# A hybrid decoder block in one kernel: the SSD branch's norm moved beside GLA, its CB mask, z product and transfer order changed

## The chip, the cores and the metric

The kernel runs on one core of a Trainium2 chip. The core has five engines with an instruction queue each: TensorE (PE) for matmuls and transposes, VectorE (DVE), ScalarE (ACT), GpSimd (POOL) and SyncE (SP), which here only issues transfers (DMA). Each engine takes its queue strictly in order; a wait at its head holds all that is behind it. The metric is the device time of one execution in microseconds. Lines such as L51 are lines of the kernel before.

## What is computed

A decoder block over 1024 tokens with a width of 1024, all in float32. Two branches read the same normed input and are merged, then come attention to a memory of 256 tokens and a gated feed-forward layer. The change concerns the first branch, the SSD (Mamba-2) mixer, and the stage of the second (GLA, gated linear attention):

```python
proj = n @ w_in
z, xBC, dt_raw, q, k, v, r, a1, g_ssd, g_gla = split(proj)
# SSD: B, C for 2 groups of 8 heads, 128 states; x has 16 heads of 64
xBC = silu(conv(xBC));  xs, Bm, Cm = split(xBC)
y = sum over s <= l of (C_l . B_s) * exp(a_cs_l - a_cs_s) * (x_s dt_s)   # plus the carried state
y = (y + D_skip * xs) * silu(z)
y_ssd = y * rsqrt(mean(y*y over each group of 512 channels) + EPS) * ssd_norm
y_gla = gla(q, k, v, r, a1, ...)
merged = sigmoid(g_ssd) * (y_ssd @ w_up_ssd) + sigmoid(g_gla) * (y_gla @ w_up_gla)
h = h + merged @ w_o
```

## The kernel before, in words

**Layout.** All activations stand transposed: channels on the 128 partitions, tokens along the row. Float32 precision comes from a split of every matmul operand into a high and a low part (`whi`, `wlo`, B11h, B11l and so on): ACT writes the high part (L220), DVE subtracts it from the source for the low one (L221), and three matmuls are made of each product.

**Units.** The projection by `w_in` is cut into units of 256 output channels. A unit (class Unit, L272) loads 1 MB of weights (`raw`, L286), and makes seven block products in the manner of Strassen, named B11, T2, T1, B21, T3, B22, T4 in the order of SPACED (L40). Each is 12 matmuls of 128x512 into one accumulator of PSUM (`acc`, four of them). A product's result is moved or added into `o` by ACT (L349, L351) or DVE, and the finished quarters are stored (`store_rows`, L465). The units come in the order zu (z, silu, stored in `sz_d`), xu (convolution), ru, qk, gs, gg. `singles` (L454) runs units one after another and gives each the next one to load; `group` asks for it at product n ≥ `frm`, which was always 6.

**Fillers.** `run` (L433) draws a generator of side work at a given rate between the products. Beside ru, qk and gs0 stands the SSD scan (391 to 640 us), beside gs1 to gg2 the GLA scan (645 to 790 us). The order of instructions on each engine, SP too, is set by a scheduler, which takes them by readiness and priority in its own model of time; a filler has a raised priority.

**The SSD scan** (class SSD, L859 to L946) has 16 steps, 8 chunks of 128 tokens times 2 groups. `load` fetches x, B, C, the sums for the decay (`csb`, a broadcast row) and silu(z). `lay` makes CB, masks it on DVE into `cbm`, transposes B (to `bt`) and x. `decay` makes `e` on ACT (eight relus, an exponential) and the exponential of `csb`, and on DVE the products e by cbm and csb by C. `scan` makes the output and the new state on PE. `gate` adds D·x on DVE, multiplies by z on POOL (L929), squares on ACT and adds up on DVE. `stat` sums over the partitions by a matmul with ones, and takes the root as a power on POOL (`rs`); `norm` spreads the 128 factors over the partitions by a matmul (`bank<-ident,rs`), multiplies on DVE (`y<-y,bank`) and stores to `ys_d`. `bank` tiles are four buffers of PSUM that all these share. `ssd_steps` sets the order: load(i+1), scan(i); stat(i−1), lay(i+1); gate(i); norm(i−1), decay(i+1).

**Later.** `fetch` (L1200) reads `ys_d` for the product with `w_up_ssd`, applying the gain `ssd_norm` on the way.

Of the kernel before, what the change touches and what calls it, by code (L numbers as in the profile page):

```python
# [16 lines left out]
P = 128  # L17
# [5 lines left out]
EPS = 1e-6  # L23
# [55 lines left out]
def block_kernel(ctx: ExitStack, tc: tile.TileContext, t: dict, out: bass.AP):  # L79
# [38 lines left out]
    kT_d = dram("kT_d", D, MEM)  # L118
    vm_d = dram("vm_d", MEM, D)
    cs_d = dram("cs_d", P, P)  # L120

    def acc():
        return ps.tile([P, 512], F32, name="acc", tag="acc", bufs=4)
# [36 lines left out]
    for a in range(2):  # L160
# [9 lines left out]
    mhalf = cp.tile([P, 8], F32, name="mhalf")  # L170
    POOL.memset(mhalf, -0.5)

    gcol, at = {}, 0
# [277 lines left out]
        for _ in g:  # L451
            pass

    def singles(units, B, then=()):  # L454

        for u, nxt in zip(units, list(units[1:]) + [None]):
            yield from group([u], B, [nxt] if nxt else then)

    def store_rows(dst, func=None):

# [257 lines left out]
    ebm = ep.tile([P, 4, NCH], F32, name="ebm")  # L718
    ebl = ep.tile([P, 4, NCH], F32, name="ebl")
    ewl = ep.tile([P, 4, NCH], F32, name="ewl")  # L720

    def conv(u, unit):
        cv = cvp.tile([P, 2, TOK], F32, name="cv", tag="cv", bufs=2)
# [114 lines left out]
    prep = chain([ssd_prep(), gla_prep()])  # L838
    run(singles(zu, B, xu[:1]), (prep, .3))
    drain(prep)  # L840
    st2.close()
    st2 = ExitStack()
    cvp = pool("conv", 1, stack=st2)
# [17 lines left out]
    class SSD:  # L861
# [8 lines left out]
        def load(s):  # L870
            g, tk = s.g, s.tk
            s.L = sp_.tile([P, 8, CH], F32, name="xz", tag="xz", bufs=3)
            SP.dma_start(s.L[:, 0:4], xbc_d[g * 512:(g + 1) * 512, tk].rearrange("(k p) s -> p k s", p=P))
            s.BC = sp_.tile([P, 2, CH], F32, name="bc", tag="bc", bufs=2)
            for i in range(2):
                r0 = 1024 + i * 256 + g * P
                SP.dma_start(s.BC[:, i], xbc_d[r0:r0 + P, tk])
            s.csb = sp_.tile([P, GH, CH], F32, name="csb", tag="csb", bufs=2)
            SP.dma_start(s.csb.rearrange("p h s -> p (h s)"),
                         cs_d[s.i0:s.i0 + GH, :].rearrange("h s -> (h s)").partition_broadcast(P))  # L880
            SP.dma_start(s.L[:, 4:8], sz_d[g * 512:(g + 1) * 512, tk].rearrange("(k p) s -> p k s", p=P))

        def lay(s):
            p = bank()
            PE.matmul(p[:, :P], s.BC[:, 0], s.BC[:, 1], start=True, stop=True)
            PE.transpose(p[:, P:2 * P], s.BC[:, 0], ident)
            s.cbm = sp_.tile([P, CH], F32, name="cbm", tag="cbm", bufs=2)
            mul(DVE, s.cbm, p[:, :P], triu)
            s.bt = sp_.tile([P, P], F32, name="bt", tag="bt", bufs=2)
            ACT.activation(s.bt, p[:, P:2 * P], AF.Copy)  # L890
            p = bank()
            for k in range(4):
                PE.transpose(p[:, k * P:(k + 1) * P], s.L[:, k], ident)
            s.xd = sp_.tile([P, GH, 64], F32, name="xd", tag="xd", bufs=2)
            mul(DVE, s.xd, p.rearrange("p (h d) -> p h d", d=64), s.heads(dt_h, 64))

        def decay(s):
            s.e = sp_.tile([P, GH, CH], F32, name="e", tag="e", bufs=2)
            for h in range(GH):
                ACT.activation(s.e[:, h], s.csb[:, h], AF.Relu, bias=cs[:, s.i0 + h:s.i0 + h + 1], scale=-1.0)  # L900
            ACT.activation(s.e, s.e, AF.Exp, scale=-1.0)
            ACT.activation(s.csb, s.csb, AF.Exp)
# [21 lines left out]
        def gate(s):  # L924
            s.y = sp_.tile([P, 4, CH], F32, name="y", tag="y", bufs=3)
            for k in range(4):
                DVE.scalar_tensor_tensor(s.y[:, k], s.L[:, k], dcol[:, s.g * 4 + k:s.g * 4 + k + 1],
                                         s.py[:, k * P:(k + 1) * P], ALU.mult, ALU.add)
            mul(POOL, s.y, s.y, s.L[:, 4:8])  # L929
            sq = sp_.tile([P, 4, CH], F32, name="sq", tag="sq", bufs=1)  # L930
            ACT.activation(sq, s.y, AF.Square)
            s.rd = sp_.tile([P, CH], F32, name="rd", tag="rd", bufs=2)
            add(DVE, sq[:, 0:2], sq[:, 0:2], sq[:, 2:4])
            add(DVE, s.rd, sq[:, 0], sq[:, 1])

        def stat(s):
            p = bank()
            PE.matmul(p[:, :1], s.rd, ones[:, :1], start=True, stop=True)
            s.rs = sp_.tile([P, 1], F32, name="rs", tag="rs", bufs=2)
            rsqrt(s.rs, p[:, :1], 1.0 / 512)  # L940

        def norm(s):
            p = bank()
            spread(p, s.rs, 1)
            mul(DVE, s.y, s.y, p[:, :P].unsqueeze(1).to_broadcast([P, 4, CH]))
            SP.dma_start(ys_d[s.g * 512:(s.g + 1) * 512, s.tk].rearrange("(k p) s -> p k s", p=P), s.y)  # L946

    def ssd_steps():
        it = [SSD(c, g) for c in range(NCH) for g in range(2)]
        it[0].load()  # L950
        yield
        it[0].lay()
        yield
        it[0].decay()
        yield
        for i in range(len(it) + 1):
            z = it[i - 1] if i else None
            a = it[i] if i < len(it) else None
            b = it[i + 1] if i + 1 < len(it) else None
            if b:  # L960
                b.load()
            if a:
                a.scan()
            yield
            if z:
                z.stat()
            if b:
                b.lay()
            yield
            if a:  # L970
                a.gate()
            yield
            if z:
                z.norm()
            if b:
                b.decay()
            yield

    ssd = ssd_steps()
    run(singles(ru + qk + gs[:1], B, gs[1:2]), (ssd, 16 * 4 / 63), prio=PRIO)  # L980
    drain(ssd)
    st3.close()

# [117 lines left out]
                c.load()  # L1101
            yield

    gla = gla_steps()
    run(singles(gs[1:] + gg[:3], B, gg[3:]), (gla, 8 * 5 / 36), prio=PRIO)
    drain(gla)
    st4.close()
    st_early.close()

# [90 lines left out]
    def fetch(src, dst, gain=None):  # L1200
# [12 lines left out]

    def fetch_gated(src, gate_src, dst):
# [9 lines left out]
                split(g, x[:, 0, half(j)], x[:, 1, half(j)])  # L1224
                yield

    get_ys = fetch(ys_d, i_ys, "ssd_norm")
    for n, _ in enumerate(group(gg[3:], B)):
        if n == 0:
            left.load(1)  # L1230
# [450 lines left out]
```

## Time and profile before

| what | us |
| --- | --- |
| median of 3 runs | 1971.84 (1967.83 to 1972.51) |
| the profiled execution | 1969.8 |
| its span in the trace | 1968.1 |
| PE busy | 1921.3 |
| DVE busy | 1312.9 |
| ACT busy | 859.9 |
| POOL busy | 599.7 |

All durations are of one profiled execution. Busy times are of instructions; matmuls are pipelined, so the sum of their busy times, or the end of one, says less than the distance of their starts. A wait is written as `engine tile line <- releaser`, a transfer as `to<-from`. The columns of a window row are its bounds and length, the busy time of PE, weight loads, DVE, ACT and POOL with the number of instructions, the granted clock of PE as a share of the full one, the DMA share, and GB/s. In an instruction's row the first two numbers are its start and its duration; what is in brackets at the end is idle time just before it and what ended it.

### The profile page before, as it was taken

What the parts mean: (1) busy time and instruction counts of PE and PEld (TensorE: products, weight loads), DVE (VectorE), ACT (ScalarE), POOL (GpSimd) and SP (SyncE); (2) the same over time, 40 slices, a digit from 0 to 9 for tenths busy, and PEclk for the clock granted to TensorE, in tenths of its full rate; (3) what the DMA queues carried; (4) which work ended last, traced back from release to release, by engine and by line L of the source; (5) the groups of instructions that cost most, each with busy time, mean ns of one, the idle gap of its engine ahead of it and who ended that gap; (6) DMA issues with size and microseconds to landing.
All of it is one profiled execution on the core that took longest, in us unless ns stands there. A gap on an engine that the chain in (4) does not pass through costs nothing.

```text
span 1968.1 us, 26260 instructions
## 1 busy us (share of the span) xinstructions
PE 1921.3 (98%) x9772; PEld 1614.5 (82%) x9772; DVE 1312.9 (67%) x1851; ACT 859.9 (44%) x1503; POOL 599.7 (30%) x442
## 2 busy tenths in 40 slices
PE   8899899999999999999999999999999999999998
PEld 7898678777788888888888888878888888878887
DVE  6866679869886655575545237576877777774565
ACT  8434745465552443643224136453333333353243
POOL 1012343455553222112433000027544444320002
PEclk9999999999999999999999999999999999999999
DMA  9333333366553654897784201442233224186463
GB/s 322 131 120 100 108 120 105 116 199 192 168 173 110 216 162 123 312 382 244 252 295 148 77 22 44 139 140 81 83 118 122 81 96 145 42 290 211 160 223 124
DMA packets 236003, 309.59 MB, mean 157 GB/s; under 512 B 16714, under 2 KB 156212, under 8 KB 235876
## 3 DMA queue, kind: packets, MB, share of 16 engines
q1 hardware_dynamic: 235876, 307.92, 46.9%
q8 instruction: 77, 1.26, 0.3%
q14 instruction: 50, 0.41, 0.1%
HBM read 211.07 MB, written 96.80 MB: 156 GB/s over the span
## 4 chain that ended last, share of the span: by engine, by line
PE 76%; DVE 9%; ACT 4%; DMA 4%; issue 4%; POOL 3%; SPq 1%; POOLq 0%; DVEq 0%; ACTq 0%
PE acc L51 66%; PE bank L51 9%; DVE wlo L73 2%; DVE cv L73 2%; DVE o L73 1%; PE bank L55 1%; DMA csb<-cs_d 1%; DMA xt<-in_x_dram 1%; DMA raw<-in_w_in_dram 1%; POOL sa L73 1%; DVE hs L73 1%; DMA fr<-act_d 1%; DVE fs L73 1%; POOL raw L73 1%; ACT whi L220 1%
## 5 line engine op out<-in xcount | busy, mean ns | idle before, releaser
L51 PE MATMUL acc<-hl,wd 128*128 128x512 f32 x1920 | 438.7, 389 | 0.0
L51 PEld LDWEIGHTS acc<-hl,wd 128*128 128x128 f32 x1920 | 360.1, 188 | 74.3
L73 DVE TENSOR_TENSOR wlo<-raw,whi 128x512 fp32r<-128x512 f32 x272 | 239.4, 886 | 87.1 <-ACT whi L220 85.0
L220 ACT ACTIVATE whi<-raw 128x512 fp32r<-128x512 f32 x272 | 169.6, 628 | 243.2 <-PE acc L51 216.5
L73 DVE TENSOR_TENSOR o<-acc,o 128x512 f32<-128x512 f32 (+1 forms) x256 | 172.7, 676 | 121.3 <-PE acc L51 110.5
L73 POOL TENSOR_TENSOR sa<-raw 128x512 f32<-128x512 f32 x47 | 77.4, 1647 | 308.7 <-DMA raw<-in_w_ffn_in_dram 227.5
L51 PE MATMUL acc<-fs 128*128 128x512 f32 (+1 forms) x792 | 156.0, 356 | 1.9 <-ACT o L1576 1.8
L73 POOL TENSOR_TENSOR raw<-raw,sa 128x512 f32<-128x512 f32 x48 | 69.7, 1451 | 270.1 <-DVE wlo L73 259.1
L51 PEld LDWEIGHTS acc<-fs 128*128 128x128 f32 x792 | 130.6, 189 | 22.9 <-ACT o L1576 2.2
L220 ACT ACTIVATE fs<-fr 128x1024 fp32r<-128x1024 f32 (+1 forms) x84 | 80.0, 984 | 112.9 <-PE acc L51 39.4
L73 DVE TENSOR_TENSOR fs<-fr,fs 128x1024 fp32r<-128x1024 f32 (+1 forms) x84 | 99.9, 1219 | 38.1 <-ACT fs L220 37.7
L220 ACT ACTIVATE whi<-sa 128x512 fp32r<-128x512 f32 x96 | 60.0, 626 | 101.2 <-PE acc L51 101.1
L73 DVE TENSOR_TENSOR wlo<-sa,whi 128x512 fp32r<-128x512 f32 x96 | 82.1, 856 | 17.5 <-ACT whi L220 16.0
L73 DVE TENSOR_TENSOR wd<-raw,wd 128x1024 fp32r<-128x1024 f32 x40 | 51.7, 1295 | 50.8 <-ACT wd L220 50.7
L73 POOL TENSOR_TENSOR raw<-raw 128x512 f32<-128x512 f32 x48 | 83.5, 1739 | 3.3 <-DVE sa L73 3.2
L220 ACT ACTIVATE wd<-raw 128x1024 fp32r<-128x1024 f32 x40 | 42.3, 1059 | 91.4 <-PE acc L51 86.7
L51 PE MATMUL acc<-T1h,whi 128*128 128x512 f32 x192 | 75.9, 395 | 2.8 <-ACT whi L220 2.8
L51 PE MATMUL acc<-B21h,whi 128*128 128x512 f32 x192 | 75.5, 393 | 2.0 <-ACT o L349 2.0
L51 PE MATMUL acc<-T4h,whi 128*128 128x512 f32 x192 | 75.8, 395 | 1.7 <-DVE o L73 1.7
L51 PE MATMUL acc<-B22h,wlo 128*128 128x512 f32 x192 | 76.0, 396 | 1.2 <-DVE wlo L73 1.2
L51 PE MATMUL acc<-B11h,whi 128*128 128x512 f32 x192 | 75.7, 394 | 1.2 <-ACT whi L220 1.2
L51 PE MATMUL acc<-T3h,wlo 128*128 128x512 f32 x192 | 75.8, 395 | 0.4 <-DVE wlo L73 0.4
(386 smaller groups left out, 4670.6 us busy)
## 6 DMA issues: line engine op xcount, KB each, us to landing
raw<-in_w_in_dram SPq DMA_DIRECT2D x26, 1024.0 KB, 6.4
raw<-in_w_ffn_in_dram SPq DMA_DIRECT2D x22, 1024.0 KB, 6.6
act_d<-o SPq DMA_DIRECT2D x77, 256.0 KB, 2.1
fr<-act_d SPq DMA_DIRECT2D x35, 512.0 KB, 6.8
pre<-in_w_ffn_out_dram SPq DMA_DIRECT2D x11, 1024.0 KB, 8.0
fr<-down_d SPq DMA_DIRECT2D x20, 512.0 KB, 3.7
down_d<-pre SPq DMA_DIRECT2D x33, 256.0 KB, 3.2
raw<-in_w_xkv_dram SPq DMA_DIRECT2D x8, 1024.0 KB, 7.7
```

The lines of the kernel that those rows point to most:

```text
L51: return s.e.matmul(o, x, y, **kw)
L55: return s.e.transpose(o, x, i)
L73: return f(*a, **kw)
L220: ACT.activation(hi, src, AF.Copy)
```

## The change

1. The norm leaves the scan. `stat` and `norm` of each step go; the sums of squares of four steps stand in one tile (`rdt`), and `stat(q)` makes their four matmuls with ones every fourth step and puts scale and epsilon on, into `ysum` (128x16). `ys_d` is stored before the norm. A new filler `ssd_norm` runs beside GLA: one power on POOL, one transpose, a store to `rs_d`, then for each of 16 blocks of 128x512 a load, one DVE instruction (factor and gain together), and a store; the factors come back as four broadcasts of 128x512. `fetch` no longer applies the gain.
2. CB is masked in `decay`, into a free part of its own PSUM bank, and the e product reads it there, ahead of the product of csb.
3. The product by z is DVE's, not POOL's.
4. The squares stand in x's own tile; B and C come in one transfer, three buffers; `csb` has its own loading step.
5. During the scan SP issues in program order (`manual_schedule`), not in the scheduler's; the next unit's weights are asked for from product 1 on (`frm=1`); the loads go two steps ahead, and the step order is load_cs(i+1), load(i+2), store(i−1), lay(i+1); scan(i); stat, gate(i); decay(i+1).
6. `settle_all()` after the preparations' drain.

Cut to its core:

```diff
-            SP.dma_start(s.L[:, 4:8], sz_d[...])
+            SP.dma_start(s.BC, xbc_d[1024:1536, tk].rearrange("(i g p) s -> g p i s", g=2, p=P)[g])
+            SP.dma_start(s.L[:, 4:8], sz_d[...])
+        def load_cs(s):
             s.csb = sp_.tile([P, GH, CH], F32, name="csb", tag="csb", bufs=2)
...
-            s.cbm = sp_.tile([P, CH], F32, name="cbm", tag="cbm", bufs=2)
-            mul(DVE, s.cbm, p[:, :P], triu)
...
+            cbm = s.p[:, 2 * P:3 * P]
+            mul(DVE, cbm, s.p[:, :P], triu)
+            mul(DVE, s.e, s.e, cbm.unsqueeze(1).to_broadcast([P, GH, CH]))
             mul(DVE, s.csb, s.csb, s.BC[:, 1].unsqueeze(1).to_broadcast([P, GH, CH]))
-            mul(DVE, s.e, s.e, s.cbm.unsqueeze(1).to_broadcast([P, GH, CH]))
...
-            mul(POOL, s.y, s.y, s.L[:, 4:8])
+            mul(DVE, s.y, s.y, s.L[:, 4:8])
...
-        def norm(s):
-            p = bank()
-            spread(p, s.rs, 1)
-            mul(DVE, s.y, s.y, p[:, :P].unsqueeze(1).to_broadcast([P, 4, CH]))
+    def stat(q):
+        p = bank()
+        for n in range(4):
+            PE.matmul(p[:, n:n + 1], rdt[q][:, n], ones[:, :1], start=True, stop=True)
+        DVE.tensor_scalar(ysum[:, 4 * q:4 * q + 4], p[:, :4], 1.0 / 512, EPS, ALU.mult, ALU.add)
...
-    run(singles(ru + qk + gs[:1], B, gs[1:2]), (ssd, 16 * 4 / 63), prio=PRIO)
+    with tc.manual_schedule(engines={mybir.EngineType.SP}):
+        run(singles(ru + qk + gs[:1], B, gs[1:2], frm=1), (ssd, 16 * 4 / 63), prio=PRIO)
...
+    def ssd_norm():
+        POOL.tensor_tensor(ysum, ysum, mhalf, ALU.pow)
+        p = bank()
+        PE.transpose(p[:NH, :P], ysum, ident)
+        rt = gl.tile([NH, P], F32, name="rt", tag="rt")
+        DVE.tensor_copy(rt, p[:NH, :P])
+        SP.dma_start(rs_d, rt)
+        yield
+        for g in range(2):
+            for j in range(2):
+                rb = gl.tile([P, 4, P], F32, name="rb", tag="rb")
+                SP.dma_start(rb, rs_d.rearrange("(c g) s -> g c s", g=2)[g][4 * j:4 * j + 4].partition_broadcast(P))
+                for k in range(4 * g, 4 * g + 4):
+                    y = gl.tile([P, HALF], F32, name="yn", tag="yn", bufs=2)
+                    rows = ys_d[k * P:(k + 1) * P, half(j)]
+                    SP.dma_start(y, rows)
+                    DVE.scalar_tensor_tensor(y, y, col("ssd_norm", k), rb.rearrange("p c s -> p (c s)"), ALU.mult,
+                                             ALU.mult)
+                    SP.dma_start(rows, y)
+                    yield
+    gla, late = gla_steps(), ssd_norm()
+    run(singles(gs[1:] + gg[:3], B, gg[3:]), (gla, 8 * 5 / 36), (late, 0.55), prio=PRIO)
...
-            if gain:
-                ACT.activation(x[:, 0], raw, AF.Copy, scale=col(gain, k))
-                DVE.scalar_tensor_tensor(x[:, 1], raw, col(gain, k), x[:, 0], ALU.mult, ALU.subtract)
-            else:
-                ACT.activation(x[:, 0], raw, AF.Copy)
-                sub(DVE, x[:, 1], raw, x[:, 0])
+            ACT.activation(x[:, 0], raw, AF.Copy)
+            sub(DVE, x[:, 1], raw, x[:, 0])
```

More of the change, by code (lines that the diff above doesn't have):

```diff
@@ L452, in drain, with singles @@
             pass
-    def singles(units, B, then=()):
+    def singles(units, B, then=(), frm=6):
         for u, nxt in zip(units, list(units[1:]) + [None]):
-            yield from group([u], B, [nxt] if nxt else then)
+            yield from group([u], B, [nxt] if nxt else then, frm=frm)
     def store_rows(dst, func=None):
@@ L955, in ssd_steps @@
         yield
[L956 to L959, printed above, removed]
+        for i, a in enumerate(it):
+            b, d = get(i + 1), get(i + 2)
             if b:
[L961 to L966, printed above, removed]
+                b.load_cs()
+            if d:
+                d.load()
+            if i:
+                it[i - 1].store()
             if b:
@@ L969, in ssd_steps @@
             yield
-            if a:
-                a.gate()
+            a.scan()
             yield
-            if z:
-                z.norm()
+            if i and i % 4 == 0:
+                stat(i // 4 - 1)
+            a.gate()
+            yield
             if b:
@@ L1198, in block_kernel, with fetch @@
     i_ys, i_yg, i_wo, i_xq, i_q, i_xo = (paired(x) for x in (EVEN, ODD, EVEN, ODD, EVEN, EVEN))
-    def fetch(src, dst, gain=None):
+    def fetch(src, dst):
         for k in range(NB):
```

41 lines of the change are left out of this document (23 added, 18 removed).

## The prediction

> **What bounds the kernel now.** I read the busy shares and the clock first, then the busy time by stage, then what TensorE (PE) waits for.
>
> ```profile
> PE 1921.3 (98%) x9772; PEld 1614.5 (82%) x9772; DVE 1312.9 (67%) x1851; ACT 859.9 (44%) x1503; POOL 599.7 (30%) x442
> ...
> PEclk9999999999999999999999999999999999999999
> ...
> 395.00:645.00 250.00, 245.11 (x1510) 199.69 (x1509) 197.84 (x327) 127.48 (x273) 127.83 (x101) 1.00 0.56 170
> 645.00:790.00 145.00, 145.00 (x725) 124.08 (x724) 85.07 (x175) 69.03 (x174) 35.76 (x28) 1.00 0.51 160
> ...
> 450.00:500.00 50.00, 49.16 (x328) 40.30 (x327) 45.42 (x74) 28.12 (x63) 26.83 (x21) 1.00 0.65 196
> ```
>
> PE is busy for 98% of 1968.1 us; a gain must either take PE instructions away or close gaps between them. The window rows give, behind the stretch and its length, the busy time of PE, weight loads, DVE, ACT and POOL, then granted clock, DMA share and GB/s. The change touches two stages. In the SSD scan (395 to 645) PE lacks 4.9 us of 250; in the GLA stage (645 to 790) it lacks nothing, so the second stage has nothing to give and can only lose. DVE is the second engine: 45.42 of 50 us in the middle of the scan.
>
> The waits of PE in the scan, in total, with count and longest:
>
> ```profile
> PE bank L51 <- POOL rs L73: 2.9, 3, 1.1
> PE bank L51 <- DVE y L73: 1.2, 3, 0.4
> ```
>
> The first two, 4.1 us in 6 waits, belong to the norm: the spread matmul waits for POOL's power, and a bank is not free until DVE has multiplied y by it. The change removes that step from the scan.
>
> **The change part by part.** The sum is made against the profiled execution: 1969.8 us, span 1968.1, 2.0 us below the median of the three runs (1971.84).
>
> *Norm taken out of the scan.* Each of the 16 steps loses a spread, DVE's product and POOL's power and gets back no PE work (the 16 one-column matmuls with ones remain, four at a time).
>
> ```profile
> L51 PE MATMUL bank<-ident,rs x32: 270/274/377, 427.4 to 637.3; 128*128 128x128 f32 x32
> ...
> 391.63 0.39 PE L51 MATMUL acc<-T4h,whi 128*128 128x512 f32 x1
> ...
> 394.12 0.39 PE L51 MATMUL acc<-T4h,wlo 128*128 128x512 f32 x1
> 394.35 0.39 PE L51 MATMUL acc<-B11h,wlo 128*128 128x512 f32 x1
> ...
> 397.07 0.39 PE L51 MATMUL bank<-bc 128*128 128x128 f32 x2
> 397.30 0.27 PE L55 MATMUL bank<-ident,bc 128*128 128x128 f32 x1
> ...
> 397.76 0.47 PE L51 MATMUL acc<-T2h,wlo 128*128 128x512 f32 x1
> ```
>
> Matmuls are pipelined, so what one costs is the distance of the starts: twelve products take 394.35 − 391.63 = 2.72 us, 0.227 each, though each is shown with 0.39. A 128-wide product in two records costs 397.30 − 397.07 = 0.23. So 16 spreads are worth 16 × 0.23 = **−3.7**. The 6 waits go: −4.1, and in each the 0.39 − 0.23 = 0.16 us for which PE shows busy while it can't start, −1.0: together **−5.1**. If another wait takes their place, this term is nothing; that is a rival. A single transpose of the 128x16 sums comes back, and the fill of the next bank around it: **+0.3**.
>
> *z's product on DVE, CB masked late, sq in place.* Busy time and mean by group, then idle before it and its releasers:
>
> ```profile
> L73 DVE TENSOR_TENSOR e<-e,cbm 128x1024 f32<-128x1024 f32 x16 | 30.5, 1906 | 2.1 <-ACT e L901 1.6
> ...
> L73 DVE TENSOR_TENSOR csb<-csb,bc 128x1024 f32<-128x1024 f32 x16 | 20.1, 1254 | 4.7 <-ACT csb L902 4.6
> ...
> L73 DVE TENSOR_TENSOR y<-y,bank 128x512 f32<-128x512 f32 x16 | 10.8, 676 | 0.9 <-PE bank L51 0.9
> ...
> L73 POOL TENSOR_TENSOR y<-y,xz 128x512 f32<-128x512 f32 x16 | 25.1, 1566 | 16.0 <-DVE rs L73 13.7 <-DVE y L73 2.4
> ...
> L890 ACT ACTIVATE bt<-bank 128x128 f32<-128x128 f32 x16 | 4.4, 276 | 49.1 <-DVE cbm L73 49.1
> ```
>
> DVE loses 16 products y by bank (10.8 us) and takes 16 of z, of the same shape, at the same 676 ns: its load in the scan doesn't change. POOL loses 25.1 us and was not the bound. The e product reads its mask from PSUM; the product y by bank, half its size, also reads PSUM and costs 676, just over half of 1254, so I price this at nothing. Bounds: −10.4 us of DVE, if the 652 ns by which e's product exceeds csb's go with POOL's product, to +10.4 if the read from PSUM costs as much again; both lie beside PE unless DVE is late, which is rival 3. The 49.1 us for which ACT's `bt` waited on DVE's mask go, but no row shows that PE waits for `bt`. I take 0.
>
> *The hand-made order at the scan's start.* Here I expect the largest loss. Until 388 us both programs queue the same instructions on every engine. SyncE (SP) issues in order:
>
> ```profile
> 369.85 0.38 SPq L286 DMA_DIRECT2D raw<-in_w_in_dram  x1
> 388.13 0.32 SPq L734 DMA_DIRECT2D xbc_d<-cv  x1
> 390.44 0.37 SPq L873 DMA_DIRECT2D xz<-xbc_d  x1
> 391.94 0.43 SPq L879 DMA_DIRECT2D csb<-cs_d  x1
> ```
>
> Before, the 1 MB of weights for unit ru1 is asked for at 369.85, ahead of the convolution's last stores, and is there when ru0 ends. In program order it is queued behind the store at 388.13 and the loads of steps 0 and 1. Working the queue forward by 0.32 to 0.5 us an issue, and with the second step's load of xz held until the store has landed (2.7 us by its group, so 390.8), `csb` is issued at 389.9 and the weights at about 392.7. They land after:
>
> ```profile
> raw<-in_w_in_dram SPq DMA_DIRECT2D x26, 1024.0 KB, 6.4
> xbc_d<-cv SPq DMA_DIRECT2D x12, 512.0 KB, 2.7
> 419.55 5.29 DMA csb<-cs_d
> 432.85 4.69 DMA csb<-cs_d
> 397.40 2.45 ACT L900 ACTIVATE e<-csb,cs 128x128 f32<-128x128 f32 x8 [2.45 <-DMA csb<-cs_d]
> 400.87 1.28 ACT L901 ACT_TABLE_LOAD   x1
> 402.17 1.06 ACT L901 ACTIVATE e<-e 128x1024 f32<-128x1024 f32 x1
> 403.26 1.36 DVE L73 TENSOR_TENSOR e<-e,cbm 128x1024 f32<-128x1024 f32 x1 [1.56 <-ACT e L901]
> ```
>
> PE runs ru0's last product from 391.2 (the two B11 matmuls that came before it, 0.46, move behind) to 393.9, then the `lay` of steps 0 and 1 (397.76 − 397.07 = 0.69 each), then the first scan matmuls, which need `e`; ru1's first product is queued behind two of them. `csb` lands 4.7 to 5.3 after its issue, at 394.6 to 395.2; relus 2.45, table 1.28, exponential 1.06, product 1.36 give 400.8 to 401.4. The weights come at 392.7 + 6.4 = 399.1, and their split stands on ACT behind the second exponential: 401 to 402 too. So PE is idle from 393.9 to 401.1 less 1.4: **+5.8**, of which 4.5 in one piece. Bounds 4.5 (the faster landing, relus that begin as the load arrives) to 8 (a 1 MB load as the fifth of a burst).
>
> *The clock after it.*
>
> ```profile
> 236.50 0.39 PE L51 MATMUL acc<-T2h,wlo 128*128 128x512 f32 x1
> 239.68 0.50 PE L51 MATMUL acc<-T1h,whi 128*128 128x512 f32 x1 [2.79 <-ACT whi L220]
> 241.81 0.63 PE L51 MATMUL acc<-T1h,wlo 128*128 128x512 f32 x1
> 245.18 0.39 PE L51 MATMUL acc<-T1l,whi 128*128 128x512 f32 x1
> 240.00:250.00 10.00, 9.21 (x34) 7.10 (x33) 10.00 (x10) 4.35 (x9) 8.82 (x5) 0.83 0.65 202
> ```
>
> After an idle time of 2.79 us, eight starts from 241.81 to 245.18 take 3.37 us in place of 8 × 0.227 = 1.82; the window's granted clock is 0.83. A stall of 4.5 us should do it once: **+1.6** (0 to 3.2). The Trainium skill ("TensorE: Matmul & The Clock Gate", Part 1) has a window of about 3.4 us that must be idle before the clock is halved, and as long a busy one to bring it back. The second half agrees with the 3.37 us here; the first does not, since 2.79 us sufficed. By either, the expected stall is long enough.
>
> *The norm's pass beside GLA.* 16 blocks are loaded, multiplied on DVE and stored through two buffers, with four broadcasts through one. A 256 KB load of this kind and a store's landing:
>
> ```profile
> ga<-h_d SPq DMA_DIRECT2D x32, 256.0 KB, 2.8
> DMA to landing us min/median/max: 2.3/2.3/2.3
> L73 DVE SCALAR_TENSOR_TENSOR qk<-qk,e x8: 691/693/1609, 646.2 to 749.5; 128x512 f32<-128x512 f32 x8
> ```
>
> Load 2.8, product 0.7 and store 2.3 with three issues of 0.4 make 7.0 us a buffer, 3.5 a block, and each of the three later broadcasts waits for its buffer and lands as `csb` does, some 5 us. Sixteen blocks want 16 × 3.5 + 3 × 5 = 71 us; the program's queue places them over some 59 us of PE's work. DVE and SP, both in order, then hold the splits, accumulations and GLA loads queued behind them for 12 us in all. The splits run two products ahead (2 × 2.72 = 5.4), and the parts overlap in the queues. I take **+3**, between 0 and 14. The loss of the gain in the fetch of ys takes nothing from PE: 0.
>
> Sum: −3.7 − 5.1 + 0.3 + 5.8 + 1.6 + 3 = +1.9, so 1971.7 on the profiled execution's scale; forecast **1971.5 us**.
>
> **The rivals.**
>
> 1. *Slower: the norm's pass holds the queues.* If each late block stops DVE ahead of a split, the 12 us of deficit and a first round trip of 2 show in PE, in place of 3: 1971.5 − 3 + 14 = **1983**. It decides once DVE falls more than 5.4 us behind between 700 and 760. Against it: DVE is busy for 85 of 145 us and DMA for 0.51. For it: SP is in order, and a store there waits for DVE ahead of GLA's own loads.
> 2. *Faster: no stall at the start.* If the weights and `csb` come before ru0 ends, or the scheduler's order leaves other matmuls in front, 5.8 + 1.6 go; with the pass hidden as well: 1971.5 − 7.4 − 3 = **1961**. For it: issue times in SP are my reckoning, and the convolution may end earlier with SP relieved.
> 3. *The change doesn't do what it says.* With DVE at 45.42 of 50, the waits of the spread turn into waits of the e product for z's, and −5.1 doesn't come: 1971.5 + 5.1 = **1976.6**. For it: all 16 products of z now stand in DVE's queue ahead of the next step's. Against it: the norm's product left that queue.
>
> **How the numbers follow.** Forecast 0.42, rival 1 0.23, rival 2 0.20, rival 3 0.15. A measurement of this kernel tells 0.3%, 5.9 us, from no change. Rival 2 and the forecast's lower tail give faster 0.23; rival 1 and half of rival 3 give slower 0.30; the rest, 0.47, is within. The range reaches from rival 2 to rival 1, and leaves a tail beyond each: 1961 to 1984; the forecast's own is 1966 to 1977.
>
> **What would show it.** Right: between 393 and 402 PE idles about 6 us in two pieces, released by ACT or DVE on `e` or by the split of ru1's weights, with a granted clock under 1 just behind; no wait on `rs` remains; PE's busy time in the scan's window falls by the spreads; between 645 and 790 PE shows a few waits where it had none. Wrong: weights that land before 394, waits of PE on `wlo` or `o` of over 6 us in GLA, or gaps on `e` or `csb` in every scan step.

## The result, and the profile after

The changed kernel takes 1987.58 us (median of 4 runs, 1986.61 to 1988.63) against 1970.46 (4 runs, 1967.83 to 1972.51): a ratio of 1.0091, 95% interval 1.0078 to 1.0104. It is slower by 17 us, where 1971.5 and "within 0.3%" had been forecast, and lies 3.6 us beyond the range. Its profiled execution took 1988.63 us, with a span of 1986.9.

Page of the changed kernel, and its windows (columns as before), with the stages and the start of the scan:

```profile
PE 1932.3 (97%) x9741; PEld 1619.3 (81%) x9741; DVE 1309.6 (66%) x1856; ACT 860.3 (43%) x1503; POOL 563.1 (28%) x411
```

```profile
395.00:645.00 250.00, 242.61 (x1464) 195.05 (x1463) 184.42 (x310) 130.32 (x277) 94.43 (x73) 0.99 0.59 181
650.00:700.00 50.00, 47.65 (x233) 40.04 (x233) 33.33 (x65) 21.78 (x51) 10.33 (x8) 0.97 0.79 255
700.00:750.00 50.00, 47.88 (x233) 39.66 (x232) 32.95 (x70) 23.02 (x61) 11.63 (x10) 0.99 0.67 220
400.00:420.00 20.00, 16.35 (x114) 12.48 (x113) 18.10 (x24) 15.97 (x32) 11.47 (x8) 0.83 0.49 159
450.00:500.00 50.00, 50.00 (x296) 40.50 (x295) 35.85 (x60) 26.07 (x58) 14.41 (x12) 1.00 0.48 149
```

PE now lacks 7.4 us of 250 where it lacked 4.9, and in the GLA stage, where it lacked nothing, 4.5 in 100 us. DVE, at 45.42 of 50 before, is at 35.85, so it has not become the bound.

The waits of PE, from 380 to 650 and from 650 to 830:

```profile
PE bank L51 <- DVE e L73: 3.6, 1, 3.6
PE bank L51 <- DMA bc<-xbc_d: 2.8, 2, 2.3
PE acc L51 <- DVE o L73: 1.7, 2, 1.0
```

```profile
PE bank L51 <- ACT whi L221: 3.7, 2, 2.3
PE acc L51 <- ACT whi L221: 0.5, 1, 0.5
PE bank L55 <- ACT o L1067: 0.2, 1, 0.2
```

No wait on `rs` is left. Waits on `e` and `bc` have come, and in GLA waits that the view puts down to ACT's `whi`.

To divide the 18.8 us by which the spans differ, take the last matmul of ru0 (ahead of the scan), of gs1 (behind it) and of gg2 (behind GLA). In the kernel before the first starts at 394.12 (its row stands in the prediction); the others, and the three of the changed kernel:

```profile
644.00 0.39 PE L51 MATMUL acc<-T4h,wlo 128*128 128x512 f32 x1
799.12 0.39 PE L51 MATMUL acc<-T4h,wlo 128*128 128x512 f32 x1
```

```profile
395.78 0.39 PE L51 MATMUL acc<-T4h,wlo 128*128 128x512 f32 x1
650.52 0.39 PE L51 MATMUL acc<-T4h,wlo 128*128 128x512 f32 x1
813.44 0.39 PE L51 MATMUL acc<-T4h,wlo 128*128 128x512 f32 x1
```

| stretch | before | changed | difference |
| --- | --- | --- | --- |
| up to ru0's end | 394.1 | 395.8 | +1.7 |
| scan, to gs1's end | 249.9 | 254.7 | +4.9 |
| GLA, to gg2's end | 155.1 | 162.9 | +7.8 |
| the rest | 1169.0 | 1173.5 | +4.5 |

(In the kernel before, two matmuls of ru1 come ahead of ru0's last product; after the change they follow it, which moves 0.5 us between the first two rows.) ru0's end doesn't divide these two rows safely. Five kernels of the next section that have the changed code up to gs1's end (e1, e2, e5, e8, e9) end ru0 at 392.8 to 394.5, but gs1 at 649.6 to 650.8, as the changed kernel does: what ru0 gains, the stall behind it loses. So the two rows are taken together, +6.5 us. The last stretch holds nearly the same code, and its 4.5 us are not explained. In it PE has one wait in the feed-forward layer that is 1.8 us long in the trace before and 3.4 here, with a lower clock behind the longer one. It is 3.2 to 4.2 us long in e1, e4, e5 and e7 and 1.2 to 2.0 in e2, e3, e8 and e9; no run shows why. What belongs to the change for certain is the middle: 6.5 us up to gs1's end and 7.8 in GLA.

**The scan's start** went as forecast. The chain of waits of the changed kernel, start, length, what:

```profile
392.29 5.19 DMA csb<-cs_d
...
397.50 2.45 ACT e L901 x8
...
402.53 1.23 DVE e L73
...
403.90 2.70 PE bank L51 x8
```

Between the rows shown stand the table load and the exponential, 1.28 and 1.06 us. From csb's issue at 392.29 to the product's end the chain is 11.5 us long, forecast 10.9 to 11.5; all of it lies 2 us later, as ru0's end does. SyncE issued ru1's weights behind two steps' loads, and PE waited for `bc` and for `e`:

```profile
394.43 0.53 SPq L287 DMA_DIRECT2D raw<-in_w_in_dram  x1
```

```profile
399.22 0.49 PE L51 MATMUL bank<-bc 128*128 128x128 f32 x2 [2.29 <-DMA bc<-xbc_d]
...
403.90 0.69 PE L51 MATMUL bank<-e,xd 128*64 128x128 f32 x4 [3.65 <-DVE e L73]
```

2.29 + 3.65 = 5.9 us of idle time, forecast 5.8. The first piece is a wait for the second step's B and C, which the forecast had not named. Behind the stall the granted clock is 0.83 in 400 to 420: the matmuls from 403.90 to 407.38 take 3.48 us by their starts, and the same shapes from 415.73 on some 1.9, so the clock costs about 1.6 us (an estimate), as forecast.

**GLA** shows rival 1. DVE's and SyncE's rows around 690 us, then PE's:

```profile
687.02 0.75 DVE L73 SCALAR_TENSOR_TENSOR yn<-yn,cols,rb 128x512 f32<-128x512 f32 x1 [0.92 <-DMA yn<-ys_d]
...
695.59 0.75 DVE L73 SCALAR_TENSOR_TENSOR yn<-yn,cols,rb 128x512 f32<-128x512 f32 x1 [1.36 <-DMA yn<-ys_d]
696.26 0.72 DVE L73 COPY_PREDICATED attm<-triu,bank 128x512 f32<-128x512 int32 x1
```

```profile
688.05 0.38 SPq L1131 DMA_DIRECT2D ys_d<-yn  x1
691.93 0.32 SPq L1128 DMA_DIRECT2D yn<-ys_d  x1
```

```profile
697.08 0.81 PE L51 MATMUL bank<-v,attm 128*128 128x256 f32 x2 [2.35 <-ACT whi L221]
```

The block of 687.02 is stored at 688.05; its buffer is loaded again at 691.93, as soon as the store has landed, and DVE takes it at 695.59: a round trip of 8.6 us, forecast 7.0 without a broadcast. (The other buffer's seven round trips, three broadcasts among them, take 8.2 on average, from 660.76 to 718.45.) The mask of GLA's attention stands behind it in DVE's queue and ends at 696.98; PE, whose wait the view puts down to ACT's `whi`, starts at 697.08. Of the 7.8 us that GLA lost, 4.4 stand in PE's waits; the granted clock of 0.97 and 0.99 in the two windows is worth another 2.0 of the 100 us (an estimate), and the forecast had no clock term here.

### The profile page after: what moved, and what is told of

Its sections match the earlier page's. It is cut to its first block, busy times and chain, and to the rows that moved or that the text cites. A ratio compares the mean times of both kernels' runs of the same rounds, so it can differ in the third digit from the quotient of the medians.

```text
span 1986.9 us, 26226 instructions
## 1 busy us (share of the span) xinstructions
PE 1932.3 (97%) x9741; PEld 1619.3 (81%) x9741; DVE 1309.6 (66%) x1856; ACT 860.3 (43%) x1503; POOL 563.1 (28%) x411
## 4 chain that ended last, share of the span: by engine, by line
PE 78%; DVE 8%; DMA 5%; ACT 3%; issue 3%; POOL 2%; SPq 1%; POOLq 0%; DVEq 0%; ACTq 0%
PE acc L51 68%; PE bank L51 9%; DVE wlo L73 2%; DVE cv L73 1%; PE bank L55 1%; DVE o L73 1%; DMA xt<-in_x_dram 1%; DVE fs L73 1%; DVE hs L73 1%; DMA yn<-ys_d 1%; DMA fr<-act_d 1%; DMA ys_d<-yn 1%; ACT whi L221 1%; POOL raw L73 0%; POOL ssum L73 0%
## 5 line engine op out<-in xcount | busy, mean ns | idle before, releaser
L51 PE MATMUL acc<-B21h,wlo 128*128 128x512 f32 x192 | 76.2, 397 | 0.0
```

Source lines behind the costliest of these rows:

```text
L51: return s.e.matmul(o, x, y, **kw)
```

## The experiments

Times are medians; the kernel before was run again beside each group of kernels (1969.6 to 1971.7).

**e1: the pass's product on GpSimd.**

```diff
-                    DVE.scalar_tensor_tensor(y, y, col("ssd_norm", k), rb..., ALU.mult, ALU.mult)
+                    mul(POOL, y, y, rb.rearrange("p c s -> p (c s)"))
```

> The changed kernel, with the multiplication of each block in the norm's pass moved from VectorE to GpSimd (the gain goes back into the fetch of ys, as before the change). Theory A, VectorE is held: in its queue each block's product waits for the block's load, and the masks, splits and accumulations behind it make TensorE wait. Then the loss of TensorE between 650 and 730 us, 8.0 us by its starts in the changed kernel, falls to 1 to 3, and the time by 5 to 7, to about 1981. Theory B, the transfers are the cause (GLA's loads and the weights come later because SyncE waits at the stores): the loss stays at 6 to 8 and the time within 2 us of the changed kernel's 1987.6.

1991.91 (1986.58 to 1994.23): nothing won. PE now waits 5.8 us in 650 to 760 for ACT's `o`, whose scale factor comes from a power on GpSimd that stands behind the blocks. Theory A in its first form falls.

**e2: no blocks.**

```diff
-            for j in range(2):
+            for j in range(0):
```

> The changed kernel without the 16 blocks of the norm's pass and its four broadcasts: the power, the transpose and the store of the factors stay, the norm of the SSD branch is left out of the result. Both theories on the GLA stage: its loss of 8.0 us goes to 0.8 or less, as before the change; the time falls by 7 to 8, to about 1980. If it falls by less than 5, the cost of the pass is not where its waits stand. What is then left over the kernel before (about 9 us) belongs to the scan and to what the trace shows outside both stages.

1977.21, 10.4 us less; PE has no wait at all from 650 to 830. By the traces the GLA stretch falls from 162.9 to 155.1 us, its length before the change, so 7.8 us are the price of the pass in its stage; most of what goes beyond that lies in the last stretch (1169.2 us, as before), where neither kernel runs the pass.

**e3: the scheduler's order for SyncE.**

```diff
-    with tc.manual_schedule(engines={mybir.EngineType.SP}):
+    if True:
```

> The changed kernel with SyncE's order in the scan left to the scheduler again (the manual order taken away, all else as changed). Theory A, the hand-made order costs the stall at the scan's start because the 1 MB of weights of ru1 is issued at 394 us: in the scheduler's order they are issued ahead of the convolution's last store, TensorE's loss in 380 to 420 us falls from 9.3 to about 3, and the time by 5 to 7, to about 1981. Theory B, the later loads of the scan profit from the hand-made order by as much: the stall goes, but waits of the same size come in 420 to 640 and the time stays within 2 us of 1987.6.

2004.91, 17 us more. The stall at the start goes, as A has it, but PE waits 9.2 us for x's loads, up to 5.2 at a time; SyncE stands 52.0 us at these loads until the squares' sums, which now lie in x's tile, are made. Both theories miss the size: with the changed step order the scheduler's order costs more than the hand-made one.

**e4: early weights.**

```diff
+    ru[1].load()
     with tc.manual_schedule(engines={mybir.EngineType.SP}):
```

> The changed kernel with one line more: the load of ru1's weights is asked for ahead of the manual order, so that the scheduler may place it before the convolution's last stores. Theory A: the weights are there by 394 us, ru1's first product follows ru0's last one, and the 6.3 us stall with its spell of half clock (together 6 to 8 us) goes: about 1981. Theory B, the chain from csb over the exponentials to e is what holds TensorE at that place (its first scan matmuls stand ahead in the queue): no more than 2 us are won.

1984.30, 3.3 us less. ru1's product follows ru0's at once, no wait of PE over 1.1 us is left from 380 to 650, and the scan's stretch is 246.7 us long in place of 254.7; GLA then takes 167.4 in place of 162.9, with two waits for ACT's `o` of 5.3 us together and one of 2.5. So A holds for the stall, but not for the time, since half of the gain is lost beside the pass.

**e5: the pass without products.**

```diff
-                    DVE.scalar_tensor_tensor(y, y, col("ssd_norm", k), rb..., ALU.mult, ALU.mult)
```

> The changed kernel with the 16 multiplications of the norm's pass left out: the blocks and the broadcasts are loaded and stored as before, so that the norm of the SSD branch is missing from the result. With GpSimd in VectorE's place the loss stayed (1991.9 against 1987.6), without the blocks 10.4 us went (1977.2). Theory A, amended: what costs is an instruction that waits for a block's load at the head of a strictly ordered compute queue, whichever engine's: with no such instruction left the time falls to within 2 us of that without the blocks, 1975 to 1979, and TensorE's loss between 650 and 740 us to under 1.5. Theory B: the transfers themselves, or SyncE's waits, delay GLA's own loads: the loss stays at 6 or more, the time at 1985 to 1990.

1988.54: theory A falls in its second form too. With no product there is

```profile
686.71 0.69 DVE L73 SCALAR_TENSOR_TENSOR qk<-qk,e 128x512 f32<-128x512 f32 x1 [9.47 <-DMA qk<-q_d]
```

GLA's own q is 9.5 us late for DVE. SyncE waits 18.9 us at the stores for the blocks' loads and 12.2 at loads for the stores, and q stands behind them.

**e8 and e9: an eighth of the bytes; a third buffer.**

```diff
-                    rows = ys_d[k * P:(k + 1) * P, half(j)]
+                    rows = ys_d[k * P:(k + 1) * P, j * HALF:j * HALF + 64]
```

```diff
-                    y = gl.tile([P, HALF], F32, name="yn", tag="yn", bufs=2)
+                    y = gl.tile([P, HALF], F32, name="yn", tag="yn", bufs=3)
```

> The changed kernel with each block of the norm's pass cut to 64 of its 512 columns: as many transfers, waits and products, an eighth of the bytes of the blocks (7 MB less); seven eighths of ys go without the norm. Without products the loss in GLA stayed (1988.5), without the blocks it went (1977.2). Theory C, bytes: the blocks' 8.4 MB beside GLA's own 16 MB in 90 us make every landing later (3.0 to 3.6 us for a block against 2.0 to 2.8): the loss falls to 2 or less, the time to 1977 to 1980. Theory D, SyncE's queue: GLA's own loads stand behind stores that wait for a block's load, however small: the loss stays at 5 or more, the time at 1984 or more.

> The changed kernel with three buffers for the blocks of the norm's pass in place of two (the transposed factors are held in the broadcast's tile to make room). As many bytes; SyncE waits less often for a buffer. Theory D, SyncE's queue: TensorE's loss in 650 to 740 us, 8.4 us by its starts, falls by 3 or more, the time to 1984 or less. Theory C, bytes: it stays within 2 us of 1987.6.

1984.06 and 1982.01. In both traces the last stretch is some 4 us shorter than in the changed kernel, with the shorter wait in the feed-forward layer, so the GLA stage is compared by itself. The window from 640 to 760, in which PE was busy throughout before the change, in the changed kernel, e8 and e9:

```profile
640.00:760.00 120.00, 114.75 (x555) 95.64 (x554) 80.35 (x158) 52.64 (x128) 28.81 (x23) 0.99 0.74 238
```

```profile
640.00:760.00 120.00, 115.41 (x562) 97.50 (x561) 74.07 (x161) 53.71 (x132) 28.22 (x23) 0.99 0.57 177
```

```profile
640.00:760.00 120.00, 115.81 (x566) 98.70 (x565) 82.96 (x166) 54.79 (x135) 29.61 (x24) 0.99 0.74 237
```

With an eighth of the bytes the DMA share is back at 0.57, and PE still lacks 4.6 us, where the changed kernel lacks 5.3: theory C falls. The third buffer wins 1.1 of them. From gs1's end to gg2's end e8 takes 161.1 us and e9 159.9, in place of 162.9: by this measure the third buffer wins 3.0 of 7.8, the least that theory D had put on it. The round trip is made of latencies more than of bytes. The blocks' transfers in the changed kernel and in e8, KB each and us to landing, 650 to 740:

```profile
ys_d<-yn SPq DMA_DIRECT2D x16, 256.0 KB, 3.6
yn<-ys_d SPq DMA_DIRECT2D x14, 256.0 KB, 3.2
```

```profile
ys_d<-yn SPq DMA_DIRECT2D x16, 32.0 KB, 2.2
yn<-ys_d SPq DMA_DIRECT2D x14, 32.0 KB, 3.3
```

A load of an eighth takes as long, a store 1.4 less. (With the third buffer, in e9, each takes 4.2 us.) What stays through e1, e5, e8 and e9 is that some in-order queue stands at the head of each round trip. That this is the cause is argued from the four together; no kernel gave the pass's transfers a queue of their own, which would have tested it. The Trainium skill ("DMA: Bandwidth & Descriptors", "Anatomy of one DMA — SWDGE (gpsimd) path") gives a fixed part of about 2.0 us, mostly the write's receipt, for transfers that GpSimd issues. Here SyncE issues them: the 2.2 us of a 32 KB store is near that figure, the 3.3 us of a 32 KB load is not. In the same section the Trainium skill has any wait of a transfer made by the engine that issues it; SyncE's waits in e5 agree.

**e6: the norm in the fetch, with early weights.**

```diff
+            r = rbp.tile([P, 4, P], F32, name="rb", tag="rb", bufs=3)
...
+                DVE.scalar_tensor_tensor(g, raw[:, half(j)], col("ssd_norm", k), rb[j]..., ALU.mult, ALU.mult)
+                split(g, x[:, 0, half(j)], x[:, 1, half(j)])
```

> The changed kernel with early weights for ru1 as in the run before, and with no pass at all: the factor and the gain are applied where ys is fetched for the product with w_up_ssd (one VectorE product and a split of each half block there, the four broadcasts loaded on the way). The whole computation is made. Theory A: the stall at the scan's start and the loss in GLA both go; the scan ended 2.5 us ahead of the kernel before with early weights, GLA loses 0.8 as before, so that the time is 1967 to 1970, 1 to 4 us under the kernel before. Rival: what the pass cost beside GLA comes back beside gg3 and the first dense layer (16 more products of 0.75 us and 8 more splits on VectorE and ScalarE ahead of that layer's operands): 1975 or more.

2002.33: in the rival's range, but by one transfer, not by the products and splits that the rival names. The fourth broadcast needs the first one's buffer and was issued at 830.70, behind the next layers' loads; PE stood 12.57 us, with shorter waits and a granted clock of 0.78 to 0.91 behind it up to 900. x2 below, which differs in a fourth buffer for the broadcasts (taken from a later pool) and in the order of the fetch's loads, takes 30.8 us less. The wait:

```profile
841.51 2.34 PE L51 MATMUL acc<-hl,wd 128*128 128x512 f32 x4 [12.57 <-ACT hl L221]
```

**s1: the kernel before without the norm.**

```diff
-            rsqrt(s.rs, p[:, :1], 1.0 / 512)
+            DVE.tensor_scalar(s.rs, p[:, :1], 1.0 / 512, EPS, ALU.mult, ALU.add)
...
-            spread(p, s.rs, 1)
-            mul(DVE, s.y, s.y, p[:, :P].unsqueeze(1).to_broadcast([P, 4, CH]))
```

> The kernel before with the norm left out of the scan and nothing in its place: no power on GpSimd, no spread by TensorE, no product by VectorE, the matmul with ones stays; the result lacks that norm's root. The prediction's term for this was -3.7 for the 16 spreads and -5.1 for the waits of the spread, -8.8 in all: about 1962. Rival, other waits take the place of those on rs: only the spreads are won, or less: 1967 or more.

1964.49 against 1971.73: −7.2, forecast −8.8. By itself the first part's gain is there, and the waits that remain in its scan come to 0.6 us in all.

**e7: z back on GpSimd.**

```diff
-            mul(DVE, s.y, s.y, s.L[:, 4:8])
+            mul(POOL, s.y, s.y, s.L[:, 4:8])
```

> The changed kernel with z's product back on GpSimd, all else as changed. If VectorE in the scan is a bound (45.4 of 50 us busy before the change), TensorE's loss in 420 to 660 us, 18.2 us in the changed kernel, falls by 2 or more and the time with it, to 1985 or less. If z's product on GpSimd makes y late for its store and its squares, or does nothing for TensorE, the time stays within 2 us of 1987.6 or rises.

1988.88, 1.3 more: z's engine decides nothing for the time.

**b1 and b2: the first part alone, in two forms.** Both are the kernel before with each step's sums written to a column of `ysum` and ys stored before the norm. b2 has the change's pass; b1 has e6's fetch with four buffers for the broadcasts.

```diff
-            rsqrt(s.rs, p[:, :1], 1.0 / 512)
+            n = 2 * s.c + s.g
+            DVE.tensor_scalar(ysum[:, n:n + 1], p[:, :1], 1.0 / 512, EPS, ALU.mult, ALU.add)
```

> The kernel before, its scan and its scheduler's order, with one part of the change in another form: the norm leaves the scan (each step's matmul with ones writes its sums to a column of one tile), one power, one transpose and one store follow beside GLA, and factor and gain are applied where ys is fetched, with all four broadcasts loaded ahead into buffers of their own (the pool of later blocks has five buffers in place of six). The whole computation is made. If leaving out the norm is worth 7.2 us in time (1964.5 against 1971.7 in the run without it) and the fetch hides 16 products of 0.75 us and 8 more splits beside gg3: 1963 to 1967, faster than both kernels. Rival: in the fetch 12.6 us were lost to one broadcast that stood behind 15 other transfers in SyncE's queue; if the operands of the first dense layer come late without that too: 1970 or more.

> The kernel before with part 1 of the change alone: the norm leaves the scan as in the run before, and the pass of 16 blocks runs beside GLA as in the change; scan order, z's product, mask and SyncE's order are those of the kernel before. By the runs so far -7.2 for the scan and +10.4 for the pass: about 1975, and TensorE's loss in GLA 6 to 10 us. If it comes at 1967 or less, the pass is costly only together with the changed scan; at 1982 or more, the scan's gain is lost there too.

b1: 1963.93 against 1969.58 (8 and 12 runs), ratio 0.9969, interval 0.9958 to 0.9979: faster than both kernels. From ru0's end to gs1's end it takes 240.8 us, against 249.9 before:

```profile
393.15 0.39 PE L51 MATMUL acc<-T4h,wlo 128*128 128x512 f32 x1
633.92 0.39 PE L51 MATMUL acc<-T4h,wlo 128*128 128x512 f32 x1
```

b2: 1978.07, 8.5 us more than the kernel before. The scan's gain of 9 us is in its trace, and GLA takes 169 us in place of 155, with a wait of 4.5 us for ACT's `o` and one for DVE's `o`. So the pass costs more, not less, without the rest of the change: b2 takes 14.1 us more than b1.

**x1, x2, x3: which other part eats the scan's gain.** x1 is b1 with the late mask and z on DVE, by the change's own lines. x2 is the changed kernel with e4's line, no pass, and b1's fetch. x3 is x2 with one matmul of sums a step:

```diff
-            if i and i % 4 == 0:
-                stat(i // 4 - 1)
...
+            if i:
+                stat(i - 1)
             if b:
                 b.lay()
```

> The kernel before with the norm out of the scan and applied in the fetch (1963.9 in its own run), and with parts 2 and 3 of the change added: CB masked late into its bank and z's product on VectorE; SyncE's order is the scheduler's. The whole computation is made. If these two parts eat the scan's gain (VectorE busy for 45 of 50 us before): 1968 or more, and TensorE's loss in 400 to 640 us rises by 4 or more over that run. If they don't: within 2 us of 1963.9.

> The changed kernel with early weights for ru1 and no pass, factor and gain applied in the fetch with all four broadcasts ahead in buffers of their own. The whole computation is made. From the run with early weights, whose scan took 246.7 us from ru0's end to gs1's end against 249.9 before and 239.8 with the norm left out of the kernel before: about 7 us above 1963.9, 1968 to 1972. If it comes within 2 us of 1963.9, the scan's other parts cost nothing once the pass and the stall are gone.

> As the run before, but the matmul with ones is made in every step, ahead of lay, instead of four at a time every fourth step among the scan's matmuls. By the starts on TensorE such a matmul costs 0.14 us between wide ones and 0.46 between the 64-column products of the scan, 5.4 in all in the changed kernel and 2.3 with the norm left out of the kernel before: 2 to 3 us less than the run before. If the place of these matmuls doesn't matter, the time stays within 1 us of it; what is then left is SyncE's order and the waits that it brings.

x1: 1963.92, as b1. x2: 1971.57, 7.6 more, of which 6.8 in the stretch up to gs1's end (247.7 us against 240.9). x3: 1982.50, a miss for both theories: two waits for a split of weights, 8.5 us together, came up near 430 and 450, so it doesn't say what the matmuls' place among the narrow products is worth.

**x4, x5, x6: the rest by itself.** x4 is x1 with the sums four at a time; x5 is x2 with the squares in their own tile; x6 is x1 with SyncE in program order, early weights and `frm=1`.

```diff
-            sq = s.L[:, 0:4]
+            sq = sp_.tile([P, 4, CH], F32, name="sq", tag="sq", bufs=1)
```

```diff
-    run(singles(ru + qk + gs[:1], B, gs[1:2]), (ssd, 16 * 4 / 63), prio=PRIO)
+    ru[1].load()
+    with tc.manual_schedule(engines={mybir.EngineType.SP}):
+        run(singles(ru + qk + gs[:1], B, gs[1:2], frm=1), (ssd, 16 * 4 / 63), prio=PRIO)
```

> The kernel before with norm in the fetch, late mask and z on VectorE (1963.9), and with the sums' matmuls with ones made four at a time every fourth step, in the scheduler's order. A group of four cost 0.81 us between wide products in the changed kernel, four single ones 0.57; single ones between the scan's 64-column products 0.46 each. In this order the groups stand after a wide product: within 1 us of 1963.9. If it comes at 1967 or more, the grouping is what eats the scan's gain.

> The changed kernel without pass, with early weights and the norm in the fetch (1971.6), and with the squares in a tile of their own, as before the change, so that x's buffer is free once the squares' sums no longer stand in it. If the loads of x that wait for these sums are what makes TensorE wait in the scan (bc, e and the splits of weights queued behind them): 1966 to 1969. If not: within 1.5 us of 1971.6.

> The kernel before with norm in the fetch, late mask and z on VectorE (1963.9), and with SyncE in program order during the scan, the next unit's weights asked for from product 1 and ru1's ahead of it; steps and their loads as before the change. If SyncE's program order itself costs the time: 1968 or more, with waits of TensorE on bc, e or the splits in 400 to 640. If it needs the change's step order to do harm: within 2 us of 1963.9.

x4: 1964.67, within 1 us. x5: 1974.98, 3.4 more, so the squares' place is no fault. x6: 1996.82, 33 more than x1: 19 of them lie ahead of ru0's end, where the last stores of the convolution held the first loads back (x6 doesn't have the change's `settle_all()` ahead of the scan), and 15 in the scan. What SyncE waits for at the stores of the units' results, 400 to 650 us, in x1, x2 and x6 in this order:

```profile
SPq L466 <- ACT o L352: 26.2, 8, 4.3
```

```profile
SPq L466 <- ACT o L352: 65.7, 7, 13.4
```

```profile
SPq L466 <- ACT o L352: 77.0, 7, 14.0
```

In program order such a store is issued where the program has it, and SyncE stands up to 14 us for the result, with the scan's loads behind it; in the changed kernel too (65.4 us in all, 14.0 the longest). In x2's scan PE then waits 1.9 us for `bc`, 1.0 for the splits, 0.8 for `e` and 0.7 for `o`, 4.4 us in all, where x1 has 1.9. So waits explain 2.5 of the 6.8 us. The rest stands in no wait: by the distances of their starts PE's matmuls cost more, `xc` by `bt` at 0.25 us a record in place of 0.20, and the sums' single columns at 0.13 in place of 0.07. Nor is a long wait of SyncE harmful by itself: before the change it waited up to 11.1 us at the stores of `y`, and up to 10.3 at those of the units' results. Program order under the old step order (x6) and the scheduler's order under the new one (e3) are both worse than the two together.

## Why the prediction was wrong

Of the 18.8 us by which the spans differ, the sum had 1.9: it had −1.1 up to gs1's end, where 6.5 were measured, +3 in GLA, where 7.8 were, and nothing for the last stretch, where 4.5 were, which no run explains.

*The start (+5.8, clock +1.6): right.* 5.9 us of idle time and about 1.6 of lower clock; e4 takes them away with one line and shortens the scan's stretch by 8.1.

*The norm out of the scan (−3.7 and −5.1): right for that part, wrong for the change.* s1 measured −7.2, and b1's scan is 9 us shorter. But the change also orders the steps and transfers of the whole scan anew, and that order was priced at its start alone; behind the start it stood at nothing, without a reason. −8.8 + 0.3 in the sum, with the start's +7.4, would make the scan some 1 us shorter, and up to gs1's end the kernel is 6.5 longer. x1 and x4 clear the mask, z and, in the scheduler's order, the sums' grouping of it. x2 prices what is left (step order, program order, early asking for weights, B and C in one transfer, the squares' place) together at 7.6, which is the gap. How the 7.6 divide is open: step order and program order are each worse with the other's counterpart, and PE's waits account for only a third. Rival 3 had a term of this size, but put it down to DVE and z, which e7 and x1 exclude.

*z, mask, squares (0): right.* x1 shows no cost. DVE is relieved of 11 us by the `e` product, which PE doesn't see, as the forecast's bound allowed.

*The pass beside GLA (+3): the other step that failed.* It costs 7.8 us in its stage and 10.4 in time. The mechanism was rival 1's, and the forecast had reckoned the deficit, 12 us, and then let 5.4 of lead and overlap absorb most of it. The demand was sized about right: a block's load and store took 3.2 and 3.6 us in place of 2.8 and 2.3, but the 16 products with their broadcasts lie within 60.3 us (660.76 to 721.06), which with the first load and the last store's landing makes 67, where 71 had been reckoned. What failed is the absorption: the lead was not there for the mask of GLA, which DVE makes just ahead of PE. The prediction named DVE and SyncE as what is held; e1 and e5 show that GpSimd, or SyncE alone, in DVE's place costs as much.

*The range* reached to rival 1 with the rest of the sum unchanged (1983). Both misses had the same sign, with the last stretch's 4.5 us on top, and the time lies beyond. That the start came out to 0.1 us is in part luck, since one of its two waits was another than forecast.

## What to carry to other kernels

A pass that loads a block, works on it and stores it back is priced by its round trips per buffer against the time in which they must fit, and by whatever stands behind each of its waits on every in-order queue, the transfer queue too; moving the work to another engine moved the wait here. Here it was better to apply the factor where the data is loaded anyway, with all that it needs in place ahead: the same first part cost 8.5 us as a pass and won 5.7 in the fetch. A transfer queue put in program order needs its waits looked at one by one, for what stands behind each: a store whose data was 14 us away held every load behind it.

## What the runs showed of the hardware

The product of `e` by the mask, 128x1024 on DVE, takes 1906 ns on average before; in the changed kernel, with the mask in PSUM, and ahead of csb's product:

```profile
L73 DVE TENSOR_TENSOR e<-e,bank 128x1024 f32<-128x1024 f32 x16 | 19.5, 1216 | 8.5 <-ACT e L902 8.2
```

690 ns less, where no difference had been expected from the operand's place. The mean of before hides two cases. One product that starts behind a running product of GpSimd, one with GpSimd idle, and one of the changed kernel behind a running product of GpSimd:

```profile
448.28 1.30 POOL L73 TENSOR_TENSOR y<-y,xz 128x512 f32<-128x512 f32 x1 [1.69 <-DVE rs L73]
448.50 2.15 DVE L73 TENSOR_TENSOR e<-e,cbm 128x1024 f32<-128x1024 f32 x1
```

```profile
553.10 1.23 DVE L73 TENSOR_TENSOR e<-e,cbm 128x1024 f32<-128x1024 f32 x1
```

```profile
558.51 1.30 POOL L73 TENSOR_TENSOR raw<-raw 128x512 f32<-128x512 f32 x1
558.63 1.21 DVE L73 TENSOR_TENSOR e<-e,bank 128x1024 f32<-128x1024 f32 x1
```

Before, with both operands in SBUF, the 12 of 16 products that start while a GpSimd product has 0.8 us or more to go take 1.90 to 2.27 us, the other four 1.22 to 1.36. With the mask in PSUM all 16 take 1.20 to 1.22, with a running GpSimd product or without, and in e7, with z back on GpSimd, 1.21 or 1.22. It is not the order of the two products: csb's, whose operands stay in SBUF and which comes second in x1, takes 1.67 us there behind a GpSimd product that began 0.46 us ahead of it (591.37 and 591.83).

The granted clock fell after 2.35 us of idle time. PE, busy for 4.73 us of the 5 from 690 on, stood idle for 2.35 us ahead of 697.08; then the clock was low:

```profile
697.00:701.00 4.00, 3.92 (x10) 3.19 (x11) 2.35 (x4) 0.51 (x3) 2.12 (x2) 0.57 1.08 363
```

Products of two records start 0.85 us apart there, and 0.43 apart from 701.00 on.

A matmul with a single column is not free, and its price goes by its place. Between a 256-wide and a 128-wide product, in the kernel before, a pair of records starts at 458.26 and the next product at 458.40, 0.14 us later. Among the scan's 64-column products of the changed kernel:

```profile
463.40 0.39 PE L51 MATMUL bank<-csb,state 128*64 128x128 f32 x4
463.72 0.38 PE L51 MATMUL bank<-ones,rdt 128*128 128x1 f32 x2
464.03 0.43 PE L51 MATMUL bank<-e,xd 128*64 128x128 f32 x2
464.39 0.38 PE L51 MATMUL bank<-ones,rdt 128*128 128x1 f32 x2
```

Here a pair and the narrow records after it take 464.39 − 463.72 = 0.67 us, where a group of four narrow records without it takes 0.32 (463.40 to 463.72): at least 0.35 us for each single column there. It was priced at nothing. In the scheduler's order the grouping costs little (x4); among the narrow products no run prices it by itself.
